# Laying out the tiles that TensorE streams and the weight blocks it holds by their addresses modulo 512

## The chip, the cores and the metric

The kernel runs on one core of a Trainium2 chip. The metric is the device time of one execution in microseconds. Three runs of the kernel before gave 626.13, 626.18 and 630.62 us, median 626.18.

## The reference

A decoder layer on 256 tokens of width 1,024 in float32, batch 1, depth 1: a SwiGLU feed-forward, a mixing block (attention and a diagonal state-space layer side by side), and a second feed-forward, each on a normalized and modulated input. Cut to what matters:

```python
ada = silu(c) @ w_ada + b_ada                       # 1024 -> 9 x 1024: shift, scale and gate, three times
h = modulate(rmsnorm(x, norm_ffn1), sh1, sc1)
x = x + 0.5 * g1 * swiglu(h, w_ffn1_in, w_ffn1_out)  # 1024 -> 2 x 2816 -> 1024
h = modulate(rmsnorm(x, norm_mix), sh2, sc2)
q, k, v, u, ga, gs = split(h @ w_in)                 # 1024 -> 4096
y_att = moba_attention(q, k, v)                      # 8 heads of 64
y_ssm = s5_mixer(u, ...)                             # 32 groups, 64 complex states each
merged = sigmoid(ga) * (y_att @ w_br_att) + sigmoid(gs) * (y_ssm @ w_br_ssm)
x = x + g2 * (merged @ w_out)
h = modulate(rmsnorm(x, norm_ffn2), sh3, sc3)
x = x + 0.5 * g3 * swiglu(h, w_ffn2_in, w_ffn2_out)
return rmsnorm(x, norm_final)
```

## The kernel before

The activations stand transposed in the on-chip buffer: 128 channels on the partitions, 256 tokens along the row, so that one block of h is 128 x 256 float32, 1,024 bytes per partition. Weights stream from memory once, in 1 MB pieces: `load` (L198) keeps four `raw` tiles of 2,048 float32 columns in flight on SyncE's queue. Each half of a raw tile, a quantum of 128 x 1,024, is split: ScalarE rounds it into `w_hi` (L239), VectorE puts the rest into `w_lo` (L247); four of each are kept. Activations are split in the same way into a high and a low part.

A product is then three matmuls (`mm3`, L269; `proj_mm`, L440): high weight with high activation, high weight with low activation, low weight with high activation. In all three a 128 x 128 block of the weight is held by TensorE and the activation of 256 columns is streamed past it; every matmul loads its own block. `tile_b` (L430) runs 24 of them for one 128-column block of an input projection, streaming h (`h_hi`, `h_lo`), and later ssm_Pr and ssm_Pi. `proj_mm` runs 24 for one quantum of an output projection, on an act tile (`a0` to `a4`, taken in turn, L543) in the feed-forwards, or on big1 and ssm_L. In one place (L1063) the roles are exchanged and 512 columns of the weight are streamed. Right behind a feed-forward or the mixing block, two projections run on the not yet normalized x (`raw_pair`, L535): their streamed rows have 258 columns, two more for the shift, and lie in four of the act tiles. The first feed-forward starts with a projection (L579) that goes along with the arrival of the weights.

The tiles come from three pools that lie one behind the other in each partition: `const` (small tables, x itself as `xT`), `near` (the names in NEAR: ssm_G0, ssm_G1, kT, qT, ssm_Pr, ssm_Pi, big0, big1, ssm_L, h_hi, h_lo, a0 to a4, in the order in which they are first asked for) and `pool` (raw, rstd, acc, diag, at_bias, w_hi, h_t, w_lo and the rest, in that order too). A tile takes its size rounded up to 32 bytes. `sb` (L62) picks the pool by the tile's name. The order of the instructions on each engine and the semaphores come from a scheduler, except in stretches marked as set by hand.

Of the kernel before, what the change touches and what calls it, by code (L numbers as in the profile page):

```python
# [10 lines left out]
F32 = mybir.dt.float32  # L11
F32R = mybir.dt.float32r
I32 = mybir.dt.int32
# [3 lines left out]
S = 256  # L17
# [21 lines left out]
ORDERED = 2  # L39
E_ = mybir.EngineType  # L40
MAN = None

NEAR = frozenset(
    ["h_hi", "h_lo", "big0", "big1", "ssm_L", "ssm_Pr", "ssm_Pi", "ssm_G0", "ssm_G1", "kT", "qT"]
    + [f"a{i}" for i in range(5)]
)
WN = 128


@with_exitstack  # L50
def kernel(ctx, tc, T, out):
    nc = tc.nc

    const = ctx.enter_context(tc.tile_pool(name="const", bufs=1))
    near = ctx.enter_context(tc.tile_pool(name="near", bufs=1))
    pool = ctx.enter_context(tc.tile_pool(name="pool", bufs=1))
    psum = ctx.enter_context(tc.tile_pool(name="psum", bufs=1, space=bass.MemoryType.PSUM))

    def bank(i):
        return psum.tile([128, 512], F32, tag=f"bank{i}", name=f"bank{i}")  # L60

    def sb(tag, shape, dt=F32, bufs=1, name=None):  # L62
        return (near if tag in NEAR else pool).tile(shape, dt, tag=tag, name=name or tag, bufs=bufs)

    x, w_ada, w_in = T["x"], T["w_ada"][0], T["w_in"][0]
    NFF = FF // 128
# [131 lines left out]
    def load():  # L198
        while state["loaded"] < len(raw_items) and (state["loaded"] < NRAW or state["loaded"] - NRAW in done):
            i = state["loaded"]  # L200
            a, b = raw_items[i][1]
            r = sb("raw", [128, 2048], bufs=NRAW)[:, 0:a * b].rearrange("p (a b) -> p a b", a=a)
            for cs, src in raw_items[i][2]:
                nc.sync.dma_start(out=r[:, :, cs], in_=src)
            raw_tiles[i] = r
            state["loaded"] += 1

    def consume_ada(i):
        v, j = raw_items[i][3:]
        r = raw_tiles.pop(i)  # L210
        if j == 0:
            acc[v] = sb("acc", [128, D], bufs=2)
        a = acc[v]
        for k in range(2):
            cs = csil[:, 2 * j + k, 0:1]
            if j == 0 and k == 0:
                nc.vector.tensor_scalar(a, r[:, k, :], cs, None, op0=ALU.mult)
            else:
                nc.vector.scalar_tensor_tensor(out=a, in0=r[:, k, :], scalar=cs, in1=a, op0=ALU.mult, op1=ALU.add)  # L219
        if j == 3:  # L220
            ada_done(v)
# [12 lines left out]
    def split_hi(k):  # L234
        i, view = quanta[k]
        r = view(raw_tiles[i])
        a, b = r.shape[1:]
        hi = sb("w_hi", [128, 1024], F32R, bufs=NSPLIT)[:, 0:a * b].rearrange("p (a b) -> p a b", a=a)
        nc.scalar.copy(hi, r)  # L239
        state["split"] += 1  # L240
        return k, r, hi
# [52 lines left out]
    ones = const.tile([128, 128], F32, name="ones")  # L294
# [4 lines left out]
    ident = const.tile([128, 128], F32, name="ident")  # L299
# [6 lines left out]
    sel = const.tile([2, 2, 64], F32, name="sel")  # L306
    cols0 = const.tile([128, 80], F32, name="cols0")
    cols = const.tile([128, 56], F32, name="cols")
    bada = cols0[:, 0:72].rearrange("p (v k) -> p v k", k=KD)
    ldt = const.tile([128, 16], F32, name="ldt")  # L310
    norm_cols = {1: cols0[:, 72:80], 4: cols[:, 32:40], 7: cols[:, 40:48]}
    hbglu = const.tile([128, 4], F32, name="hbglu")
    dq = const.tile([128, 16], F32, name="dq")
# [613 lines left out]
    dist = const.tile([128, S], F32, name="dist")  # L927

    def attn_consts():
        di = sb("dist_i", [128, S], I32)  # L930
        nc.gpsimd.iota(di, pattern=[[-1, S]], base=128, channel_multiplier=1)
        nc.vector.tensor_copy(dist, di)
        nc.gpsimd.affine_select(
            out=dist, in_=dist, compare_op=ALU.is_ge, fill=1.0e32, base=128,
            pattern=[[-1, S]], channel_multiplier=1,
        )
# [21 lines left out]
    def warm(n):  # L958
        for _ in range(n):
            nc.tensor.matmul(warm_p[:, 0:WN], ones, ones[:, 0:1].to_broadcast([128, WN]), start=True, stop=True)  # L960

# [42 lines left out]
    ssm_L = sb("ssm_L", [128, 16, 4, 32])  # L1004
# [34 lines left out]
    qT = sb("qT", [128, 4, S])  # L1039
# [4 lines left out]
    for _ in prep:  # L1044
        pass
    attn_consts()
    for j in range(4):
        if j == 2:
            raw_pair(xg, qp[1])
        p = qp[j // 2][j % 2]  # L1050
        t = sb("act_f", [128, 2, S])[:, j % 2, :]
# [32 lines left out]
    kT = sb("kT", [128, 4, S])  # L1084
# [254 lines left out]
    nf = const.tile([128, KD], F32, name="nf")  # L1339
# [85 lines left out]
```

## Time and profile before

| | |
|---|---|
| median of three runs | 626.18 us |
| the profiled execution | 629.36 us, span 627.1 us |
| mean granted TensorE clock | 0.974 of full |
| matmuls | 5,328, each with a weight load |
| read from memory | 134.82 MB, 217 GB/s over the span |

The span is the time from the first to the last instruction of the profiled execution; its whole time has what lies around it. TensorE's time is told in two parts, matmuls (PE) and weight loads (PEld), which overlap. Two neighbouring matmuls overlap too, so the length of one is more than the distance from its start to the next start, which is called its pace here. The granted clock is the share of full speed that TensorE was allowed, 1.0 in most of the span.

### The profile page before, as it was taken

To read this page: it belongs to the slowest core of one execution; us is meant where nothing else is said; L and a number is where in the kernel's file an instruction comes from. 1 tells how busy PE (TensorE), PEld (TensorE's weight loads), DVE (VectorE), ACT (ScalarE), POOL (GpSimd) and SP (SyncE) were. 2 spreads that over 40 slices of the span, in tenths; PEclk is the share of its full clock that TensorE was granted. 3 is DMA by queue.
4 is the path that set the end of the run, shared out by engine and by line. 5 is a ranking of instruction groups with operands and counts; after the bars stand their busy time and mean duration, and the time that the engine had idled before them with its cause. 6 is when DMAs were issued, how large, how long until landed. Compare 5 with 4: busy or idle time off the path is not lost. (4 is left out here: it accounts for less than half of the span.)

```text
span 627.1 us, 12786 instructions
## 1 busy us (share of the span) xinstructions
PE 607.1 (97%) x5328; PEld 580.7 (93%) x5328; DVE 455.5 (73%) x823; ACT 324.6 (52%) x535; POOL 30.6 (5%) x44
## 2 busy tenths in 40 slices
PE   7999999999999989999979999998999999999996
PEld 7888999999999989898868899997999999999995
DVE  2599999889875587999976848977974645655543
ACT  4336855487444464662456565455644343434434
POOL 6200000020000020000000000002000000000001
PEclk8999999999999997999988999998999999999998
DMA  9999989766887644785586744582576655845301
GB/s 278 319 240 332 347 281 344 251 223 239 275 281 256 203 134 135 247 291 195 172 285 214 261 153 138 198 269 83 188 265 204 244 172 192 269 149 189 133 2 68
DMA packets 97706, 136.70 MB, mean 218 GB/s; under 512 B 7697, under 2 KB 77410, under 8 KB 97648
## 3 DMA queue, kind: packets, MB, share of 16 engines
q1 hardware_dynamic: 97360, 135.81, 64.7%
q8 instruction: 42, 0.69, 0.5%
q0 software_dynamic: 288, 0.07, 0.1%
q14 instruction: 16, 0.13, 0.1%
HBM read 134.82 MB, written 1.05 MB: 217 GB/s over the span
## 5 line engine op out<-in xcount | busy, mean ns | idle before, releaser
L247 DVE TENSOR_TENSOR w_lo<-raw,w_hi 128x1024 fp32r<-128x1024 f32 (+1 forms) x184 | 223.1, 1219 | 96.0 <-ACT w_hi L239 95.4
L239 ACT CAST w_hi<-raw 128x1024 fp32r<-128x1024 f32 (+1 forms) x184 | 189.0, 1037 | 196.2 <-PE bank L271 125.7
L270 PE MATMUL bank<-h_hi,w_hi 128*128 128x256 f32 x768 | 217.7, 284 | 0.1
L271 PE MATMUL bank<-h_lo,w_hi 128*128 128x256 f32 x768 | 216.6, 282 | 0.0
L272 PE MATMUL bank<-h_hi,w_lo 128*128 128x256 f32 x768 | 216.1, 281 | 0.0
L270 PEld LDWEIGHTS bank<-h_hi,w_hi 128*128 128x128 f32 x768 | 145.6, 190 | 2.9 <-issue 2.6
L272 PEld LDWEIGHTS bank<-h_hi,w_lo 128*128 128x128 f32 x768 | 145.7, 190 | 0.9 <-issue 0.8
L271 PEld LDWEIGHTS bank<-h_lo,w_hi 128*128 128x128 f32 x768 | 145.7, 190 | 0.7 <-issue 0.7
L443 PE MATMUL bank<-a,w_hi 128*128 128x256 f32 x352 | 99.2, 282 | 0.0
L444 PE MATMUL bank<-a,w_hi 128*128 128x256 f32 x352 | 99.0, 281 | 0.0
L445 PE MATMUL bank<-a,w_lo 128*128 128x256 f32 x352 | 98.8, 281 | 0.0
L443 PEld LDWEIGHTS bank<-a,w_hi 128*128 128x128 f32 x352 | 66.3, 188 | 1.0 <-issue 1.0
L219 DVE SCALAR_TENSOR_TENSOR acc<-raw,csil,acc 128x1024 f32<-128x1024 f32 x49 | 62.7, 1279 | 6.1 <-DMA raw<-in_w_ada_dram 5.7
L445 PEld LDWEIGHTS bank<-a,w_lo 128*128 128x128 f32 x352 | 66.2, 188 | 0.0
L444 PEld LDWEIGHTS bank<-a,w_hi 128*128 128x128 f32 x352 | 66.1, 188 | 0.0
L271 PE MATMUL bank<-a,w_hi 128*128 128x258 f32 x96 | 29.1, 303 | 5.0 <-DVE a L642 5.0
L465 POOL TENSOR_TENSOR silu<-silu,act_f 128x512 f32<-128x512 f32 x7 | 9.4, 1340 | 453.1 <-ACT act_f L463 270.7
L272 PE MATMUL bank<-a,w_lo 128*128 128x258 f32 x96 | 29.3, 305 | 0.0
L270 PE MATMUL bank<-a,w_hi 128*128 128x258 f32 x96 | 28.9, 301 | 0.0
L579 PE MATMUL bank<-h_hi,w_hi 128*128 128x256 f32 x112 | 28.0, 300 | 0.5 <-ACT w_hi L239 0.5
L579 PE MATMUL bank<-h_lo,w_hi 128*128 128x256 f32 x112 | 28.0, 289 | 0.0
L579 PE MATMUL bank<-h_hi,w_lo 128*128 128x256 f32 x112 | 27.2, 282 | 0.0
(316 smaller groups left out, 828.6 us busy)
## 6 DMA issues: line engine op xcount, KB each, us to landing
raw<-in_w_ffn_in_dram SPq DMA_DIRECT2D x36, 1024.0 KB, 5.1
raw<-in_w_ada_dram SPq DMA_DIRECT2D x28, 1024.0 KB, 5.3
raw<-in_w_ffn_out_dram SPq DMA_DIRECT2D x22, 1024.0 KB, 5.0
raw<-in_w_in_dram SPq DMA_DIRECT2D x16, 1024.0 KB, 5.5
raw<-in_w_ada_dram SPq DMA_DIRECT2D x16, 512.0 KB, 7.9
raw<-in_w_ffn_in_dram SPq DMA_DIRECT2D x8, 896.0 KB, 7.5
raw<-in_w_out_dram SPq DMA_DIRECT2D x4, 1024.0 KB, 4.8
raw<-in_w_br_att_dram SPq DMA_DIRECT2D x2, 1024.0 KB, 6.1
```

The source lines that it names most:

```text
L219: nc.vector.scalar_tensor_tensor(out=a, in0=r[:, k, :], scalar=cs, in1=a, op0=ALU.mult, op1=ALU.add)
L239: nc.scalar.copy(hi, r)
L247: nc.vector.tensor_tensor(out=lo, in0=r, in1=hi.bitcast(F32), op=ALU.subtract)
L270: nc.tensor.matmul(o, st[0], mv[0], start=first, stop=False)
L271: nc.tensor.matmul(o, st[0], mv[1], start=False, stop=False)
L272: nc.tensor.matmul(o, st[1], mv[0], start=False, stop=last)
L443: nc.tensor.matmul(mm3_o, wj[0], a[0], start=first and j % 2 == 0, stop=False)
L444: nc.tensor.matmul(mm3_o, wj[0], a[1], start=False, stop=False)
L445: nc.tensor.matmul(mm3_o, wj[1], a[0], start=False, stop=last and j % 2 == 1)
L465: nc.gpsimd.tensor_tensor(out=total, in0=total, in1=sq, op=ALU.add)
L579: nc.tensor.matmul(pb[b][:, n * S:(n + 1) * S], z[:, b * 128:(b + 1) * 128], h[hl][:, kb, :], start=(kb == 0 and n == 0 and y == 0), stop= ...
```

## The change

The pools `near` and `const` are cut into parts. The streamed tiles (h_hi, h_lo, big0, big1, ssm_L, ssm_Pr, ssm_Pi and the act tiles) go into parts `str0` to `str4`, the first with a pad of 384 bytes ahead of it. Between two act tiles a part `fill0` to `fill3` takes small constants that were in `const`. Behind `str4` a part `wts` takes a pad of 32 bytes and then w_hi and w_lo, which were in `pool`. ssm_G0, ssm_G1, kT and qT go to `pool`. The integer table dist_i (L930) no longer has a tile of its own and takes one of the three slots of h_t. No other instruction is changed.

```diff
--- before.py
+++ after.py
@@ -39,11 +39,15 @@
 ORDERED = 2
 E_ = mybir.EngineType
 MAN = None
-
-NEAR = frozenset(
-    ["h_hi", "h_lo", "big0", "big1", "ssm_L", "ssm_Pr", "ssm_Pi", "ssm_G0", "ssm_G1", "kT", "qT"]
-    + [f"a{i}" for i in range(5)]
+STREAMED = ("h_hi", "h_lo", "big0", "big1", "ssm_L", "ssm_Pr", "ssm_Pi")
+FILL = (
+    ("ones", "cols0", "ada0", "ada1", "ada2", "ada3", "ada4"),
+    ("ident", "cols", "ada5", "ada6", "ada7", "ada8", "dq", "ldt"),
+    ("sel", "hbglu", "dt", "mag", "ang", "si", "co", "a_r", "a_i"),
+    ("rows1", "nf") + tuple(f"scr{i}" for i in range(7)),
 )
+PAD0 = 384
+PADW = 32
 WN = 128
 
 
@@ -51,16 +55,43 @@
 def tile_hybrid_layer_kernel(ctx, tc, T, out):
     nc = tc.nc
 
-    const = ctx.enter_context(tc.tile_pool(name="const", bufs=1))
-    near = ctx.enter_context(tc.tile_pool(name="near", bufs=1))
-    pool = ctx.enter_context(tc.tile_pool(name="pool", bufs=1))
+
+
+    parts = {}
+
+    def part(name):
+        parts[name] = ctx.enter_context(tc.tile_pool(name=name, bufs=1))
+        return parts[name]
+
+    part("const")
+    place = {}
+    for i in range(5):
+        for t in (STREAMED if i == 0 else ()) + (f"a{i}",):
+            place[t] = f"str{i}"
+        for t in FILL[i] if i < 4 else ():
+            place[t] = f"fill{i}"
+    part("str0").tile([128, PAD0 // 4], F32, name="pad0")
+    for i in range(5):
+        if i:
+            part(f"str{i}")
+        if i < 4:
+            part(f"fill{i}")
+    part("wts").tile([128, PADW // 4], F32, name="padw")
+    place.update(w_hi="wts", w_lo="wts")
+    pool = part("pool")
+
+    class Const:
+        def tile(self, shape, dt, name):
+            return parts[place.get(name, "const")].tile(shape, dt, name=name)
+
+    const = Const()
     psum = ctx.enter_context(tc.tile_pool(name="psum", bufs=1, space=bass.MemoryType.PSUM))
 
     def bank(i):
         return psum.tile([128, 512], F32, tag=f"bank{i}", name=f"bank{i}")
 
     def sb(tag, shape, dt=F32, bufs=1, name=None):
-        return (near if tag in NEAR else pool).tile(shape, dt, tag=tag, name=name or tag, bufs=bufs)
+        return parts[place.get(tag, "pool")].tile(shape, dt, tag=tag, name=name or tag, bufs=bufs)
 
     x, w_ada, w_in = T["x"], T["w_ada"][0], T["w_in"][0]
     NFF = FF // 128
@@ -927,7 +958,7 @@
     dist = const.tile([128, S], F32, name="dist")
 
     def attn_consts():
-        di = sb("dist_i", [128, S], I32)
+        di = sb("h_t", [128, S], I32, bufs=3)
         nc.gpsimd.iota(di, pattern=[[-1, S]], base=128, channel_multiplier=1)
         nc.vector.tensor_copy(dist, di)
         nc.gpsimd.affine_select(
```

## Rows read from the trace of the kernel before

**Rows 1.** The page: busy time of each engine, its share of the span, instructions

```profile
PE 607.1 (97%) x5328; PEld 580.7 (93%) x5328; DVE 455.5 (73%) x823; ACT 324.6 (52%) x535; POOL 30.6 (5%) x44
```

**Rows 2.** TensorE's waits, the longest: total us, times, longest

```profile
PE bank L271 <- DVE a L642: 5.0, 2, 2.6
```

**Rows 3.** Stretch, length, busy us (xstarted) of PE, PEld, DVE, ACT, POOL; clock, DMA, GB/s

```profile
20.00:60.00 40.00, 38.61 (x342) 33.51 (x343) 33.06 (x142) 20.84 (x39) 1.08 (x3) 1.00 1.04 293
68.00:92.00 24.00, 24.00 (x207) 24.00 (x207) 23.96 (x45) 15.22 (x29) 0.00 (x0) 1.00 0.85 290
275.00:325.00 50.00, 47.00 (x657) 42.20 (x657) 49.12 (x86) 23.92 (x51) 0.00 (x0) 1.00 0.61 208
437.00:550.00 113.00, 113.00 (x958) 112.85 (x958) 73.77 (x91) 53.60 (x65) 0.00 (x0) 1.00 0.63 215
```

**Rows 4.** The same view: a0, a1, a2, h, a4, a1, h, a3

```profile
142.35:147.95 5.60, 5.60 (x50) 5.60 (x49) 4.47 (x5) 5.50 (x10) 0.01 (x1) 1.00 0.49 167
160.36:166.02 5.66, 5.66 (x50) 5.66 (x49) 5.66 (x9) 2.62 (x3) 0.00 (x0) 1.00 0.80 280
177.22:182.97 5.76, 5.76 (x50) 5.76 (x49) 2.63 (x3) 1.76 (x3) 0.00 (x0) 1.00 0.72 277
201.18:212.38 11.20, 11.20 (x98) 11.20 (x97) 5.24 (x6) 4.69 (x5) 0.00 (x0) 1.00 0.47 143
212.38:218.02 5.64, 5.64 (x50) 5.64 (x49) 3.74 (x4) 2.62 (x3) 0.00 (x0) 1.00 0.62 193
223.62:229.06 5.44, 5.44 (x50) 5.44 (x49) 4.61 (x11) 3.67 (x7) 0.12 (x1) 1.00 0.56 176
473.55:484.86 11.31, 11.31 (x98) 11.31 (x97) 4.90 (x4) 4.69 (x5) 0.00 (x0) 1.00 0.54 184
604.78:610.47 5.69, 5.69 (x50) 5.69 (x49) 2.51 (x3) 1.57 (x2) 0.00 (x0) 1.00 0.00 0
```

**Rows 5.** The same view, 258-column projections: a0, a2, a4

```profile
445.17:446.60 1.43, 1.43 (x14) 1.43 (x13) 1.33 (x5) 1.43 (x2) 0.00 (x0) 1.00 1.03 424
448.06:449.52 1.46, 1.46 (x14) 1.46 (x13) 1.46 (x4) 0.51 (x1) 0.00 (x0) 1.00 0.06 8
245.04:246.48 1.44, 1.44 (x14) 1.44 (x13) 1.44 (x6) 0.82 (x3) 0.00 (x0) 1.00 0.05 15
```

**Rows 6.** Matmul groups: line, out<-in, shape, count, busy us, mean ns

```profile
L270 PE MATMUL bank<-h_hi,w_hi 128*128 128x256 f32 x768 | 217.7, 284 | 0.1
L443 PE MATMUL bank<-a,w_hi 128*128 128x256 f32 x352 | 99.2, 282 | 0.0
L270 PE MATMUL bank<-a,w_hi 128*128 128x258 f32 x96 | 28.9, 301 | 0.0
L579 PE MATMUL bank<-h_hi,w_hi 128*128 128x256 f32 x112 | 28.0, 300 | 0.5 <-ACT w_hi L239 0.5
```

**Rows 7.** One line's matmuls in a window: ns min/median/max, starts

```profile
L444 PE MATMUL bank<-a,w_hi x17: 276/276/280, 223.4 to 228.8; 128*128 128x256 f32 x17
L271 PE MATMUL bank<-h_lo,w_hi x32: 277/279/281, 201.3 to 212.2; 128*128 128x256 f32 x32
L272 PE MATMUL bank<-h_hi,w_lo x1: 274/274/274, 270.2 to 270.2; 128*128 128x256 f32 x1
L837 PE MATMUL bank<-ident,big x32: 270/272/327, 98.4 to 122.8; 128*128 128x128 f32 x32
L270 PE MATMUL bank<-h_hi,w_hi x83: 277/280/388, 275.3 to 320.6; 128*128 128x256 f32 x83
```

**Rows 8.** Instructions in order of time: start us, us, engine, line

```profile
225.10 0.28 PE L444 MATMUL bank<-a,w_hi 128*128 128x256 f32 x1
225.10 0.19 PEld L445 LDWEIGHTS bank<-a,w_lo 128*128 128x128 f32 x1
```

**Rows 9.** Instructions of dist_i and of h_t, as in rows 7

```profile
L931 POOL IOTA dist_i<- x1: 353/353/353, 3.4 to 3.4; 128x256 int32 x1
L417 DVE SCALAR_TENSOR_TENSOR h_t<-xT,ada,at_bias x24: 472/478/486, 14.3 to 449.9; 128x256 f32<-128x256 f32 x24
```

## The prediction

> **What bounds the kernel.** I read the page's engine line first: TensorE is busy 97% of the span [rows 1]. Then the list of who waited for whom: its longest wait on another engine sums to 5.0 us [rows 2]. So nothing feeds TensorE late, and only the rate at which it takes matmuls can be worth much. The page's mean of 280 ns for one matmul is its length; matmuls overlap, so their pace has to come from windows that hold one sort of matmul alone. An output quantum is 16 each of L443, L444 and L445, so 48 matmuls on one act tile start in each 5.4 to 5.8 us window of [rows 4] (the counts there include two that reach in from an edge); four input quanta on h are 96. Which act tile it is follows from the code, which hands them out in turn.
>
> Window by matmuls gives: a0 5.60/48 = 116.7 ns, a1 117.9, a2 120.0, a3 118.5, a4 117.5, h 116.7 in one stretch and 117.8 in another, and a1 once 113.3 [rows 4]. The DMA shares and the ScalarE and VectorE times in those rows go up and down without the pace following them: a3 with no DMA at all is slower than a0 with half of it. What distinguishes the tiles is where they lie.
>
> **Where the operands lie, from the code.** Tiles stand in the order in which they are first asked for, rounded up to 32 bytes. In `near` all sizes are multiples of 512 up to the act tiles of 4,128 bytes (258 columns, 16 bytes each). If h lies at R modulo 512, so do ssm_G, big, ssm_L, ssm_Pr, ssm_Pi and a0, and a1 to a4 lie at R+32 to R+128. Behind a4 stand four raw tiles (multiples of 512), two rstd (64 bytes), two acc, diag and at_bias: w_hi and w_lo lie at R+160+64 = R+224, and each of their 128-column blocks is 512 bytes, so all blocks do. The block thus lies above the streamed tile by 224 bytes for h and a0, 192 for a1, 160 for a2, 128 for a3, 96 for a4. In that order the paces are 116.7 to 117.8, 117.9 (once 113.3), 120.0, 118.5, 117.5: highest at 160, falling on both sides. The projections on raw x, 258 columns, show the same order: 12 matmuls in 1.43, 1.46 and 1.44 us on a0, a2 and a4, that is 119, 122 and 120 ns [rows 5]. Their rows are 1,032 bytes long, so a4's distances there run from 96 down to 72.
>
> **The change, part by part.** *The distance becomes 64 everywhere.* const loses the small tiles; the streamed ones start behind a 384-byte pad; each act tile (4,128) is followed by 992 bytes of filling (512+320+5x32, 512+224+4x32+64+64, 512+32+7x64, 512+32+7x64), which makes 5,120, a multiple of 512. So h, big, ssm_L, ssm_Pr, ssm_Pi and a0 to a4 share one residue; behind a4 (32 over) the 32-byte pad puts w_hi and w_lo 64 above it. No matmul, split or load of weights is added or taken away.
>
> What is 64 worth? No row shows it at this pairing, so it is bounded from both sides. Below: the a1 window at 113.3 has the same code, tile and distance as windows at 117.9, so some 4.5 ns of a matmul can go. Its matmuls last 276 ns against 279 on h; where the load behind a matmul on h is of ssm_G, at distance 0, the matmul lasted 274 [rows 7], 2 ns less again, which makes 111.3 the lower bound. Above: a2's 120.0. The nearest rows argue for opposite ends: distance 0 (274 ns) for a free stream, a4's 72 to 96 in the raw projections (120 ns, no better than a0's 119) for no gain. Transposes of big, which lies 64 above ident, decide nothing: their 128 columns last 272 ns, as long as 256 do here [rows 7]. I take 113.3: 64 is nearer to 0 than to a4's 96 or the peak at 160, and near 0 both reads begin almost together (a matmul and the load for the next start within 10 ns of each other [rows 8]) and the stream, moving twice as far in the same time (1,024 bytes against 512), runs away from the block, while from farther below it has to overtake it (an argument, which no row shows).
>
> *How many matmuls gain.* Streamed through weights: 3x768 on h, 3x352 on a, 3x112 in the first projection and 3x96 of 258 columns [rows 6]; from the code 3x64 on big and ssm_L and 3x32 on ssm_Pr and ssm_Pi; together 4,272. Left out: the 336 of L579, which run while DMA is at 1.04 and above; some 120 after them up to 92 us (207 start in the stretch from 68, the first 85 still of L579), and 3x83 between 275 and 325 us, stages in which VectorE is busy 23.96 of 24.00 and 49.12 of 50.00 us [rows 3, 7] and would take over as the bound. That leaves about 3,566: some 2,270 on h and its like, 1,008 on a, 288 of 258 columns.
>
> *The sum.* h from 117.2 (middle of its two paces) to 113.3: 2,270 x 3.9 = 8.9 us. a from 118.1 (mean of 116.7, 117.9, 120.0, 118.5, 117.5) to 113.3: 1,008 x 4.8 = 4.8 us. Raw projections by some 5 ns: 288 x 5 = 1.4 us. Together 15.1 us. The profiled execution took 629.4 us (span 627.1), 3.2 more than the median of 626.2; taken from it the sum gives 614.3, from the median **611.1**. What would be late next: VectorE, at 73.77 of 113.00 us, and DMA, at 0.63, have room in the longest stage [rows 3].
>
> *dist_i moves into a slot of h_t.* Its iota (353 ns) ran on GpSimd at 3.4 us [rows 9], with VectorE's cast behind it, while x was still landing; the first h_t is written at 14.3 us [rows 9], so a slot is free then: 0. If the iota were put behind h_t's other users, the cast would hold VectorE's queue, and the splits behind it, for 0.35 us and the semaphores: under 1 us. *Constants, ident, ssm_G, kT, qT and raw at new addresses*: same instructions, so 0; at most some 3 ns, what tile and tile differ by above, on the 1,056 other matmuls of 5,328 [rows 1], 3 us either way.
>
> *A rule against it.* The window rows show a pace that differs from tile to tile, 116.7 against 120.0, with the same matmul. The Trainium skill, "TensorE: Matmul & The Clock Gate", in the step-by-step of a matmul, says that the moving operand and the weight load have two independent read ports and that loading the next weights takes no bandwidth from the running matmul. By that rule no distance could matter and the sum would be 0, 626.2 us; the trace does not agree as far as tiles go, since a2 costs 3.3 ns more than a0.
>
> **The rivals.** *Levelled only (same):* 64 is no better than 224, and all the change does is to bring a1 to a4 to h's pace. For it: a4 at 96 runs at h's pace (117.5), and in the raw rows at 96 to 72 a4 is no faster than a0 at 224. Price: 1,008 x 0.9 + 288 x 1.4 = 1.3 us, 624.9. *No effect (same):* the pace depends on something other than the distance; a1's two paces at one distance speak for it, the order of the tiles in both tables against. 626.2. This is also what the page's rule above would give. *A worse meeting (slower):* at 64 the two reads meet as at 160, and every stream runs at a2's pace. Price: 2,270 x 2.8 + 1,008 x 1.9 + 288 x 1.5 = 8.7 us, 634.9. It decides from a rise of 1.8 ns on 3,566 matmuls, 6.3 us, that is from 119.2 ns on h. For it: the paces are not monotonic in distance, and 64 was never tried; against: falling from 160 to 96.
>
> **Numbers.** Free stream 0.47, levelled only 0.27, no effect 0.09, worse meeting 0.17. The likeliest gives 611, its own range 603 (111.3 ns, and the left-out stages gain too) to 619 (half the gain). The whole range: 600, the lower bound on all 4,272 (x 6.1 = 26 us), to 631, which holds both cases of no change and a worse meeting of about 1.4 ns; it leaves out most of the slower case. A measurement of this kernel can tell about 1%, 6.3 us, from no change: faster 0.47, same 0.36, slower 0.17.
>
> **What would show it.** Windows of 48 on any act tile should last the same for a0 to a4, near 5.44 us, and four quanta on h 10.9 instead of 11.2; matmuls should last 274 to 276 ns. All tiles alike at 5.60 to 5.65 would mean levelling, 5.76 the worse meeting, and tiles that still differ among themselves would mean that distance modulo 512 is not what sets the pace. VectorE should idle less between 92 and 236 us. The prediction fails most simply if 64 still lies inside the reach of whatever makes 96 no better than 224.

## The result, and the profile after

The changed kernel took 624.0 us (median of 20 runs, 619.4 to 629.2), the kernel before 626.7 us beside it (20 runs, 624.1 to 631.7). The ratio is 0.994 with a 95% interval of 0.992 to 0.996: some 3 us were gained, which is real and less than 1%. The forecast was 611. The profiled execution of the changed kernel happens to be the longest of its 20 (629.18 us, span 626.9), so its total shows no gain over the profiled one before (span 627.1); it has to be read stage by stage. Line numbers are 31 higher than before.

The engine line of the page, which answers to [rows 1]:

```profile
PE 602.9 (96%) x5328; PEld 575.3 (92%) x5328; DVE 455.2 (73%) x823; ACT 325.1 (52%) x535; POOL 31.1 (5%) x44
```

TensorE is busy 4.2 us less (607.1 before), and in this execution it waits that much more. Its longest waits, to be held against [rows 2] (engine, line, what it waited for: us in total, times, longest):

```profile
PE bank L302 <- DVE a L673: 4.8, 2, 2.4
PE bank L1180 <- issue: 3.6, 2, 3.3
PE bank L399 <- DMA raw<-in_w_ada_dram: 2.6, 2, 1.6
PE bank L610 <- ACT h_hi L451: 2.3, 2, 1.7
```

The last two lie in the first stage, which goes along with the arrival of the weights. Now the windows of [rows 4] and one of [rows 5] in the changed kernel: a0, a1, a2, h, a4, a1, a1, a3, h, h, a3, with 48 matmuls on an act tile and 96 on h, and then a2 and a0 with 12 matmuls of 258 columns (columns as in [rows 3]):

```profile
142.70:148.14 5.44, 5.44 (x51) 5.44 (x49) 4.73 (x6) 5.32 (x10) 0.13 (x1) 1.00 0.47 164
160.32:165.97 5.65, 5.65 (x50) 5.65 (x49) 5.65 (x9) 2.58 (x3) 0.00 (x0) 1.00 0.86 284
178.12:183.56 5.44, 5.44 (x51) 5.44 (x49) 0.73 (x1) 1.05 (x1) 0.00 (x0) 1.00 0.99 368
201.99:213.29 11.30, 11.30 (x98) 11.30 (x97) 5.23 (x6) 4.69 (x5) 0.00 (x0) 1.00 0.52 160
213.29:218.94 5.65, 5.65 (x50) 5.65 (x49) 3.74 (x4) 2.62 (x3) 0.00 (x0) 1.00 0.60 188
224.60:230.25 5.65, 5.65 (x50) 5.65 (x49) 4.79 (x11) 3.88 (x8) 0.35 (x1) 1.00 0.57 191
485.83:491.48 5.65, 5.65 (x51) 5.65 (x49) 3.74 (x4) 2.62 (x3) 0.00 (x0) 1.00 0.58 196
519.90:525.34 5.44, 5.44 (x50) 5.44 (x49) 3.74 (x4) 2.62 (x3) 0.00 (x0) 1.00 0.51 161
525.34:536.22 10.88, 10.88 (x98) 10.88 (x97) 6.68 (x6) 4.71 (x5) 0.00 (x0) 1.00 0.58 194
559.32:570.62 11.30, 11.30 (x98) 11.30 (x97) 4.90 (x4) 4.69 (x5) 0.00 (x0) 1.00 0.50 160
604.54:610.20 5.66, 5.66 (x51) 5.66 (x49) 2.51 (x3) 1.57 (x2) 0.00 (x0) 1.00 0.00 0
...
437.57:439.01 1.44, 1.44 (x15) 1.44 (x13) 1.44 (x4) 1.43 (x4) 0.00 (x0) 1.00 0.04 11
446.17:447.61 1.44, 1.44 (x15) 1.44 (x13) 1.40 (x5) 1.44 (x2) 0.00 (x0) 1.00 1.02 421
```

In these windows two paces are left, and nothing between: 5.44/48 = 113.3 ns and 5.65/48 = 117.8. Both occur on one tile (a3 at 519.90 and at 604.54) and on h (525.34 and 559.32), so the tile no longer decides. Such a steady pace is called a rhythm here, and the first matmul behind an interruption of the stream a restart. The two rhythms hold for whole uninterrupted stretches: read from the start times of the matmuls, 452 to 514 us is 527 matmuls at 117.8, 515 to 556 is 358 at 113.3, 557 to 612 is 469 at 117.8 again. The 120.0 of a2 is gone. The raw projections stay at 1.44/12 = 120 ns. One line's matmuls in the a1 window of 224.60 and in the a3 window of 519.90 tell the two paces apart by their length (ns min/median/max, first and last start):

```profile
L475 PE MATMUL bank<-a,w_hi x16: 281/281/281, 224.4 to 229.7; 128*128 128x256 f32 x16
...
L475 PE MATMUL bank<-a,w_hi x16: 276/276/276, 520.0 to 525.1; 128*128 128x256 f32 x16
```

### The profile page after: what moved, and what is told of

It reads as the page before. It is cut to its first block, busy times and chain, and to the rows that moved or that the text cites. A ratio compares the mean times of both kernels' runs of the same rounds, so it can differ in the third digit from the quotient of the medians.

```text
span 626.9 us, 12787 instructions
## 1 busy us (share of the span) xinstructions
PE 602.9 (96%) x5328; PEld 575.3 (92%) x5328; DVE 455.2 (73%) x823; ACT 325.1 (52%) x535; POOL 31.1 (5%) x44
```

## The experiments

Two rivals stood beside the reading that 64 bytes allows two rhythms and that a restart picks one: that levelling the act tiles brought all of the gain, and that distance doesn't matter. A triple is the three matmuls of one product, a residue an address modulo 512, and a distance how far the held block lies above the streamed tile. In the code and the diffs, `...` stands for lines left out.

**Triples alone, all distances.** The kernel `sweep` only loads two streamed and two held tiles and runs the triple of `mm3`, 48 matmuls at a time:

```python
for s in SHIFTS:            # (96, 0): streamed tiles at residue 224, then 128
    for d in DISTS:         # range(0, 512, 32): held blocks d bytes above them
        for f in KICKS:     # (0, 1, 2, 3): what stands ahead of the 48
            ...
                nc.tensor.matmul(o[:, 0:c], a[:, q:q + 128], b[:, p:p + c], start=t == 0, stop=t == RUN - 1)
```

> Leaves out the whole layer: it only runs the matmul triples of the kernel (held high, high, low block; streamed high, low, high tile; 256 columns) 48 at a time, for the distances 0, 32, ... 480 bytes modulo 512 between held and streamed blocks, with the streamed tiles at two residues (224 and 128), each four times with another restart ahead of it (nothing, one matmul of 4 columns in plain float32, a shorter second matmul, two plain float32 matmuls). Two rhythms (the theory): every run of 48 goes at one of two paces, 113.3 or 117.8 ns; which of them are found depends on the distance, and for one distance on the restart; at 64 both occur, and there are distances at which only one does. Distances 128 and 160 show a third, 119 to 120 ns. The residue of the streamed tile itself changes nothing. Distance alone (rival 1): each distance has one pace, whatever the restart, with 64 somewhere between 113.3 and 117.8. Residue (rival 2): the two residues 224 and 128 give different paces at the same distance. No effect of addresses (rival 3): all 128 runs go at one pace within 0.5 ns.

Windows of 36 paces at residue 224 (columns as above). In order: distance 0; 64 twice; 96; 128; 160; 192 twice; 224 twice; 256; 320:

```profile
28.20:32.52 4.32, 4.32 (x39) 4.32 (x38) 0.00 (x0) 0.00 (x0) 0.00 (x0) 1.00 0.00 0
63.86:67.94 4.08, 4.08 (x38) 4.08 (x37) 0.00 (x0) 0.00 (x0) 0.00 (x0) 1.00 0.00 0
81.35:85.59 4.24, 4.24 (x39) 4.24 (x38) 0.00 (x0) 0.00 (x0) 0.00 (x0) 1.00 0.02 4
86.99:91.22 4.23, 4.23 (x38) 4.23 (x37) 0.00 (x0) 0.00 (x0) 0.00 (x0) 1.00 0.00 0
110.53:114.80 4.27, 4.27 (x39) 4.27 (x37) 0.00 (x0) 0.00 (x0) 0.00 (x0) 1.00 0.00 0
145.93:150.25 4.32, 4.32 (x39) 4.32 (x38) 0.00 (x0) 0.00 (x0) 0.00 (x0) 1.00 0.02 4
158.02:162.10 4.08, 4.08 (x39) 4.08 (x37) 0.00 (x0) 0.00 (x0) 0.00 (x0) 1.00 0.02 4
175.70:179.94 4.24, 4.24 (x39) 4.24 (x38) 0.00 (x0) 0.00 (x0) 0.00 (x0) 1.00 0.01 4
181.35:185.59 4.24, 4.24 (x39) 4.24 (x37) 0.00 (x0) 0.00 (x0) 0.00 (x0) 1.00 0.00 0
192.82:197.02 4.20, 4.20 (x38) 4.20 (x37) 0.00 (x0) 0.00 (x0) 0.00 (x0) 1.00 0.00 0
216.42:220.74 4.32, 4.32 (x38) 4.32 (x37) 0.00 (x0) 0.00 (x0) 0.00 (x0) 1.00 0.00 0
252.09:256.17 4.08, 4.08 (x38) 4.08 (x37) 0.00 (x0) 0.00 (x0) 0.00 (x0) 1.00 0.02 4
```

Divided by 36 this is 120.0 at 0, 113.3 or 117.8 at 64, 117.5 at 96, 118.6 at 128, 120.0 at 160, 113.3 or 117.8 at 192, 117.8 or 116.7 at 224. VectorE and ScalarE stand still and DMA all but does (a share of 0.02 at most), so what differs is the addresses and the restart alone. This is the table of [rows 4]: 120.0 on a2 at 160, 118.5 on a3 at 128, 117.5 on a4 at 96, 116.7 and 117.8 on h and a0 at 224, and the 117.9 and the single 113.3 on a1 at 192, which the prediction had used as its lower bound. One window of the kernel before, which [rows 4] leave out, has a3 at another pace, 5.76/48 = 120.0 (columns as in [rows 3]):

```profile
519.02:524.78 5.76, 5.76 (x50) 5.76 (x49) 3.74 (x4) 2.62 (x3) 0.00 (x0) 1.00 0.53 177
```

At distance 128 the triples alone have this pace too, behind one of four restarts at residue 128. The theory holds in its main point, that a distance allows certain rhythms and 64 two. It had not said that distances 256 apart are alike (0 and 256, 64 and 320), so that the period is 256 bytes and not 512, nor that 0 is as slow as 160; and it was wrong that every run but those at 128 and 160 goes at 113.3 or 117.8: 32 had 118.3 and 224 mostly 116.7. Between residues 224 and 128 the set of paces is the same at 0, 32, 64, 160 and 192; at 96 and 128 the second one shows 120.0 beside the others, and at 224 it shows 116.7 alone. Whether the residue does that or the pace of the run ahead was not separated. No effect of addresses and one pace per distance are both out; distance 32 gave 118.3.

**What picks the rhythm.** The kernel `kick` has the same triples: 33 distances in steps of 8 bytes, then distance 64 with an extra matmul of 0 to 192 columns ahead of each run of 24.

```python
if k:
    nc.tensor.matmul(banks[7][:, 0:k], st[1][:, s0:s0 + 128], mv[0][:, m0:m0 + k], start=True, stop=True)
```

> Leaves out the layer, as the first measurement of matmul triples did. First 33 distances from 0 to 256 bytes in steps of 8, each with four runs of 24 matmuls that follow an extra matmul of 0, 32, 96 or 160 columns into another bank. Then, at distance 64 alone, 104 runs of 24 in mixed order, each behind an extra matmul of 0, 4, 16, 32, 64, 96, 128 or 192 columns, 13 times each. Two rhythms, set by the restart (the theory): at 64 a run without an extra matmul keeps the pace of the run before it; an extra matmul moves it from 113.3 to 117.8 ns or back, the same way each time for one length and one pace before; a length that leads from either pace to 113.3 may exist. Of the distances between 32 and 96 some have only 113.3 (then that is where the tiles should lie) or none but 64 has it. Chance (rival): after an extra matmul of one length, from one pace, both paces follow about equally often, and 113.3 can be lost without any restart.

Windows of 12 paces: distance 8; then, at 64, runs that follow one another, behind extra matmuls of 4, 192, 0 and 96 columns:

```profile
27.90:29.28 1.38, 1.38 (x14) 1.38 (x13) 0.00 (x0) 0.00 (x0) 0.00 (x0) 1.00 0.00 0
463.09:464.50 1.41, 1.41 (x14) 1.41 (x13) 0.00 (x0) 0.00 (x0) 0.00 (x0) 1.00 0.00 0
466.01:467.37 1.36, 1.36 (x15) 1.36 (x13) 0.00 (x0) 0.00 (x0) 0.00 (x0) 1.00 0.00 0
468.73:470.09 1.36, 1.36 (x15) 1.36 (x13) 0.00 (x0) 0.00 (x0) 0.00 (x0) 1.00 0.00 0
471.61:473.02 1.41, 1.41 (x14) 1.41 (x13) 0.00 (x0) 0.00 (x0) 0.00 (x0) 1.00 0.00 0
```

117.8, then 113.3 behind the 192 columns, kept where nothing comes between (13 of 13 runs without an extra matmul keep the pace before them), and lost behind 96 columns. Over the 104 runs 113.3 was lost behind every extra matmul of 4 to 128 columns (28 of 28; the expectation of *Three distances* has this number wrong) and kept behind every one of 192 (4 of 4); from 117.8 it was found in 23 of 49 with 4 to 128 columns and 5 of 9 with 192. So the restart picks. Away from 113.3 it does so always the same way; from 117.8 one length led both ways, which the theory had excluded and its rival, chance, had not. No distance in steps of 8 had 113.3 behind all of its four restarts; 8 bytes gave 115.6 every time.

**Levelled at 224.** One number of the changed kernel is undone: the act tiles stay level, the distance goes back.

```diff
-PADW = 32
+PADW = 192
```

> One number of the changed kernel is set otherwise: the pad ahead of w_hi and w_lo is 192 bytes in place of 32, so every streamed tile lies 224 bytes below the held blocks, as h and a0 did before, and a0 to a4 are still level. Two rhythms (the theory, by which 64 gives long stretches at 113.3 ns and 224 gives 116.7 or 117.8): a1 to a4 come down to h's pace, h stays; 1,008 x 0.9 + 288 x 1.4 = 1.3 us less than before, ratio 0.998, that is slower than the changed kernel by some 2.4 us; no window of 48 on an act tile goes under 5.60 us but by chance. Levelling only (rival): all that the change brought is from a1 to a4 no longer lying at 96 to 192; ratio 0.994 as for the changed kernel, windows of 48 at 5.60 to 5.65. Distance doesn't matter at all: 1.000.

628.6 us against 628.9, ratio 0.998 (0.994 to 1.002). Windows on a1, a2 and a3:

```profile
162.56:168.16 5.60, 5.60 (x51) 5.60 (x50) 5.60 (x9) 2.63 (x3) 0.00 (x0) 1.00 0.83 264
503.02:508.62 5.60, 5.60 (x51) 5.60 (x49) 3.74 (x4) 2.62 (x3) 0.00 (x0) 1.00 0.58 189
605.40:611.00 5.60, 5.60 (x50) 5.60 (x49) 2.51 (x3) 1.57 (x2) 0.00 (x0) 1.00 0.00 0
```

116.7 on all act tiles (of the stretches of over 200 matmuls, read from the start times, those from 70 and 381 us were at 117.8, the others at 116.7): levelling works as the prediction's second case has it and is worth, as far as the interval tells, what that case said (1.3 us). The interval reaches the changed kernel's 0.994, so the times alone don't part the two; the windows do, since 113.3 is gone.

**Level at 0.** `PADW = 480` instead.

> The changed kernel with the pad ahead of w_hi and w_lo at 480 bytes in place of 32: held blocks and streamed tiles lie at one residue, distance 0 modulo 512. In the measurement of triples alone distance 0 gave 120.0 ns behind every restart. Theory (distance sets which rhythms there are, in the layer as in the triples alone): windows of 48 on any act tile last 5.76 us, four quanta on h 11.52; against the kernel before, mean 117.4 on 4,072 matmuls of 256 and 258 columns, 2.6 x 4,072 = 10.5 us more, less what stages that wait for data hide, so 8 to 10.5 us, ratio 1.013 to 1.017. Rival (levelling is all that counts): as the changed kernel, 0.994. Rival (the prediction's own argument, that the closer to 0 the freer the stream): 113.3 everywhere, 0.975.

632.4 us against 629.0, ratio 1.007 (1.004 to 1.010). Windows on a1, a1 and a3:

```profile
162.57:168.33 5.76, 5.76 (x51) 5.76 (x50) 5.58 (x8) 2.62 (x3) 0.00 (x0) 1.00 0.85 310
483.90:489.66 5.76, 5.76 (x51) 5.76 (x49) 3.74 (x4) 2.61 (x3) 0.00 (x0) 1.00 0.59 204
606.40:612.16 5.76, 5.76 (x50) 5.76 (x49) 2.51 (x3) 1.57 (x2) 0.00 (x0) 1.00 0.00 0
```

120.0 everywhere, as in the triples alone, and the sign is right; the price is not. The mean pace rose from 117.44 to 119.90 ns, which on the 4,072 matmuls of 256 and 258 columns that ran without an interruption at full clock makes 10.0 us; by the ratio 4.5 came. Part of the rest is clock: the mean granted clock was 0.989 over its 10 runs and 0.981 over the 23 of the kernel before. The two levels being 1 and 0.5, that is 14 us at half clock instead of 24. A line through those 23 runs gives 0.35 us of time for each us at half clock, so by it 3.5 us were given back. The remaining 2 us were not traced.

**The integer table alone.** The kernel before, with the diff's last hunk only: `di = sb("h_t", [128, S], I32, bufs=3)`.

> The kernel before with one part of the change alone: the integer table takes a slot of h_t; no address of a streamed or held tile is moved by it. Theory (the part is worth nothing that can be measured; the few instructions of GpSimd and VectorE that move past one another lie where TensorE has its work): ratio 1.000, within 0.002. Rival (the table's cast, now behind other users of the slot, holds VectorE's queue and with it the splits of the first stage, which after the change is some 2 us behind by 55 us): 2 to 4.7 us more, 1.003 to 1.007.

628.4 us against 629.0, ratio 0.999 (0.996 to 1.002): worth nothing that can be measured.

**An extra matmul at restarts.** The changed kernel, with 21 matmuls of 192 columns whose result is overwritten at once:

```diff
-    def tile_b(o, w, h, nk, c0=0):
+    def tile_b(o, w, h, nk, c0=0, extra=False):
         hi, lo = w
+        if extra:
+            nc.tensor.matmul(o[:, 0:192], hi[:, 0, c0:c0 + 128], h[0][:, 0, 0:192], start=True, stop=True)
...
-                        tile_b(p[:, n * S:(n + 1) * S], nextq(), h, KD)
+                        tile_b(p[:, n * S:(n + 1) * S], nextq(), h, KD, extra=p is pg and n == 0)
...
-            tile_b(p[:, c * S:(c + 1) * S], w, ya, 4, c * 128)
+            tile_b(p[:, c * S:(c + 1) * S], w, ya, 4, c * 128, extra=c == 0)
```

> The changed kernel, distance 64, with 21 extra matmuls of 192 columns that are overwritten at once: ahead of the first matmul of each group of four projections in the feed-forwards and of four in the mixing block. In the triples alone such a matmul led from 117.8 ns to 113.3 in 5 of 9 cases and left 113.3 as it was in 4 of 4. Theory (the rhythm is picked at each restart and kept; the gain that was missing is the stretches that start in the slow one, 1,747 matmuls in five long stretches): two thirds of 1,747 x 4.45 = 7.8 us come back, 5.2 us, less 21 x 0.116 = 2.4 us that the extra matmuls take; 2.8 us faster than the changed kernel, ratio to the kernel before 0.990, and most windows of 48 on act tiles between 440 and 610 us at 5.44. Rival (the pace has to do with what else goes on in the stretch, not with its start): stretches keep their paces, 2.4 us slower than the changed kernel, 0.998.

617.9 us against 629.0, ratio 0.983 (0.979 to 0.987). Windows on a1, a1, a1 and a3:

```profile
161.26:166.91 5.65, 5.65 (x50) 5.65 (x49) 5.61 (x8) 2.31 (x3) 0.00 (x0) 1.00 1.03 372
223.66:229.10 5.44, 5.44 (x50) 5.44 (x49) 4.60 (x11) 3.67 (x7) 0.12 (x1) 1.00 0.59 197
477.17:482.61 5.44, 5.44 (x50) 5.44 (x49) 3.74 (x4) 2.62 (x3) 0.00 (x0) 1.00 0.62 206
593.91:599.35 5.44, 5.44 (x50) 5.44 (x49) 2.51 (x3) 1.57 (x2) 0.00 (x0) 1.00 0.00 0
```

Work was added, and the kernel became faster than the kernel before and the changed one (ratio 0.994). By the start times 7 of the extra matmuls met a stream at 117.8, and 6 of them led to 113.3; 11 met one at 113.3, and all kept it. The stretch that was 452 to 514 us in the changed kernel turned at its first extra matmul and stayed at 113.3; the one from 158 us turned only at its second, at 184 us. It is faster than the theory's 0.990, because nearly all long stretches turned and not two thirds. That the paces belong to what else goes on in a stretch is out.

**Three distances.** In a triple three matmuls and three loads alternate, so three distances are free. The kernel `combo` tries 8 x 8 x 8 of them, each behind two restarts, with

```python
a = st[0][:, q:q + 128] if y < 2 else st[1][:, q + f // 4:q + f // 4 + 128]
b = mv[1][:, p + e // 4:p + e // 4 + 256] if y == 1 else mv[0][:, p:p + 256]
```

> Leaves out the layer, as the other measurements of triples do. Three distances are set apart from one another, each 0 to 224 bytes in steps of 32: held high block above streamed high tile, streamed low tile above streamed high tile, held low block above held high block; so far the two others were 0. Each of the 512 combinations runs 21 triples' matmuls twice, behind an extra matmul of 96 and of 128 columns (of 21 runs at 113.3 ns in the measurement with mixed order that were followed by an extra matmul of 4 to 128 columns all but none fell to 117.8). Theory (each of the three matmuls of a triple meets the load running beside it by its own distance, and the rhythm is what the three settle to): some combinations keep 113.3 or less behind both restarts, others are at 120 and above; (64, 0, 0) comes out at 113.3 or 117.8 by the restart. Rival: only the first distance counts; all 64 combinations that share it have its paces, and none keeps 113.3 always.

Windows of 12 paces: held high 64 above, held low no farther, behind both restarts; held low another 128 farther, behind both:

```profile
685.98:687.34 1.36, 1.36 (x15) 1.36 (x14) 0.00 (x0) 0.00 (x0) 0.00 (x0) 1.00 0.00 0
688.50:689.91 1.41, 1.41 (x14) 1.41 (x13) 0.00 (x0) 0.00 (x0) 0.00 (x0) 1.00 0.05 12
706.64:708.00 1.36, 1.36 (x15) 1.36 (x14) 0.00 (x0) 0.00 (x0) 0.00 (x0) 1.00 0.00 0
709.14:710.50 1.36, 1.36 (x14) 1.36 (x13) 0.00 (x0) 0.00 (x0) 0.00 (x0) 1.00 0.00 0
```

Of 512 combinations only (64, 0, 128) ran at 113.3 behind both, and only (64, 0, 0) behind one. About half of all lie at 117.9 or above. So the first distance does not settle the pace: of the 64 combinations that share 64 as the first, 62 never had 113.3, and with (64, 0, 32) the same triples ran at 118.9 behind the first restart.

**The held low blocks 128 bytes farther.** The changed kernel with that one pad, and beside it the changed kernel itself:

```diff
-    place.update(w_hi="wts", w_lo="wts")
+    part("wtl").tile([128, 32], F32, name="padl")
+    place.update(w_hi="wts", w_lo="wtl")
```

> The changed kernel with one pad more: 128 bytes between w_hi and w_lo, so that the held high blocks lie 64 bytes above the streamed tiles and the held low blocks 192 above them. No instruction is added. In the triples alone this was the one of 512 combinations that went at 113.3 ns behind both restarts. Theory (the rhythm that a stretch settles to is set by the three distances of the triple, and the missing gain is the stretches in the slow rhythm): every long stretch goes at 113.3, windows of 48 on any act tile last 5.44 us, four quanta on h 10.88; against the kernel before the 15.1 us of the prediction's sum less some for stages that don't gain, ratio 0.977 to 0.982, and some 8 us less than the changed kernel. Rival (restarts decide in the layer whatever the distances): a mix of 113.3 and 117.8 remains, ratio 0.990 to 0.997. Rival (a faster stream is given back by more half-clock time, as the slower one at distance 0 got some back): windows at 5.44, but mean clock under 0.975 and ratio 0.983 to 0.990.

> The changed kernel itself once more, on the same chip as the kernel with the extra pad. Ratio 0.994 within 0.002; long stretches at 113.3 and 117.8 mixed, and the same ones as in the first profile if what comes before a stretch picks the rhythm, others if chance does.

617.0 us against 627.6 for the kernel before, ratio 0.983 (0.978 to 0.988); the changed kernel beside it took 623.7, ratio 0.994 (0.991 to 0.997). No instruction more, and 6.7 us less than the changed kernel. Windows on a1, a1 and a3, then the first 12 and the next 12 paces of the stretch that starts at 443.75 us, and the engine line:

```profile
158.67:164.11 5.44, 5.44 (x51) 5.44 (x49) 5.44 (x9) 2.18 (x3) 0.00 (x0) 1.00 0.89 280
219.82:225.26 5.44, 5.44 (x50) 5.44 (x49) 4.61 (x11) 3.67 (x7) 0.13 (x1) 1.00 0.59 203
592.35:597.79 5.44, 5.44 (x51) 5.44 (x49) 2.52 (x3) 1.57 (x2) 0.00 (x0) 1.00 0.00 0
443.75:445.16 1.41, 1.41 (x14) 1.41 (x13) 1.41 (x5) 1.41 (x3) 0.00 (x0) 1.00 1.02 415
445.16:446.52 1.36, 1.36 (x14) 1.36 (x13) 1.36 (x4) 0.51 (x1) 0.00 (x0) 1.00 0.28 105
```

```profile
PE 591.7 (96%) x5328; PEld 565.0 (92%) x5328; DVE 455.3 (74%) x823; ACT 324.9 (53%) x535; POOL 31.0 (5%) x44
```

Every stretch of over 250 matmuls is at 113.3 to 113.5. It is not that the restarts went better: as in the last two rows of windows (117.5 ns, then 113.3), most stretches begin slowly, and all 13 of 46 matmuls and more have come down to 113.3 by their 19th pace. The slow rhythm, which the changed kernel held for 527 matmuls, does not last at these distances. The clock did not take the gain back: 0.9805 on average against 0.982.

Of the changed kernel's repetition the long stretches from 157, 198, 374, 446 and 551 us were at 117.8 and those from 133 and 508 at 113.3, as in the first profile; where in the first a wait for w_lo cut the one from 158 at 175 us and 113.3 followed, here nothing cut it and it stayed at 117.8. Two shorter ones came out the other way round than in the first profile: 47 matmuls from 127 us at 113.4 in place of 117.8, and 60 from 293 us at 117.8 in place of 113.5. So what precedes a stretch mostly picks the same rhythm for it, and not always.

## Why the prediction was wrong, step by step

**The place of the cost was right.** TensorE's pace on streamed matmuls bounds the kernel; it depends on how far the held block lies from the streamed tile; five distances explain the five tiles. The triples alone show it.

**The failing step is "What is 64 worth? ... I take 113.3".** 113.3 was taken as the pace of a distance, while it is one of two rhythms that 64 allows, and 64 had it in 36 to 39% of the matmuls on h and the act tiles (the share of those closer than 115.2 ns; 31 to 38% in the repetition). The evidence was in [rows 4], a1 with two paces at one distance, and a3 had two as well, the second in the window that the rows leave out. The text used a1's lower pace as a bound for what can go, and the pair as a point for *no effect*, and never asked what decides between them. The terms of the sum, with the mean paces from the start times in the three traces (matmuls at full clock without an interruption) and the prediction's counts:

| | matmuls | forecast | measured | with the extra pad |
|---|---|---|---|---|
| h and its like | 2,270 | 117.2 to 113.3, 8.9 us | 117.0 to 116.1, 2.1 us | 113.9, 7.0 us |
| act tiles | 1,008 | 118.1 to 113.3, 4.8 us | 117.9 to 116.2, 1.7 us | 113.7, 4.3 us |
| raw, 258 columns | 288 | 5 ns, 1.4 us | 120.5 to 119.7, 0.2 us | 120.1, 0.1 us |
| sum | 3,566 | 15.1 us | 4.0 us | 11.4 us |

4.0 us agrees with the 0.6% of the ratio, and 11.4 with the 10.6 us that the extra pad brought (617.0 against 627.6). The sum was thus worked out rightly for a kernel that keeps the fast rhythm, but for the raw projections; the change made one that has it in some stretches, by the restart. One count is off and costs 0.2 us: of the 207 matmuls from 68 us on 35 are of L579, not 85, and 48 on an act tile, so that the prediction's h is 48 too many.

**The argument for 64 was false.** "64 is nearer to 0" and "near 0 both reads begin almost together" would make 0 the best distance; it is one of the worst, 120.0 in the triples and in the layer. The 274 ns of the one matmul ahead of a load of ssm_G [rows 7] was one value, of another tile, and not a steady pace. That the pace falls on both sides of 160 was read from five points and continued to 64; in the triples it goes 118.3, 113.3 or 117.8, 117.3 to 120.0, 118.6 to 120.0, 120.0 from 32 to 160, with no slope.

**The modulus was too large.** Distances repeat after 256 bytes. It changed no number here.

**Raw projections.** The four rows of 1,032 bytes in one act tile lie 64, 56, 48 and 40 bytes below the held blocks, and levelling the first one left them at 120 ns. In the triples of 256 columns, with both streamed tiles at one distance, 56, 48 and 40 gave 117.8 and more behind each of four restarts; the mix of the four was not measured. The 1.4 us were the mean's gain put on tiles that have 64 in one row of four.

**The table's place.** The prediction has its iota at 3.4 us, where a slot is free. It went behind h_t's other users (instructions of the table in the changed kernel, columns as in [rows 9]):

```profile
L962 POOL IOTA h_t<- x1: 343/343/343, 55.5 to 55.5; 128x256 int32 x1
...
L963 DVE CAST dist<-h_t x1: 282/282/282, 72.4 to 72.4; 128x256 f32<-128x256 int32 x1
```

The prediction named this as the other possibility, at under 1 us; the run with this part alone shows 0.999.

**The rule against it.** With VectorE and ScalarE idle and DMA all but idle, the same matmuls went at 113.3 to 120.0 ns by addresses alone. The Trainium skill, "TensorE: Matmul & The Clock Gate", in "Step-by-step: what each phase is for", gives TensorE two independent read ports, one for the streamed and one for the held operand. By that rule, as the prediction read it, the kernel before and all of these would take the same time; the runs differ by 15 us, from 617.0 to 632.4 (ratios 0.983 and 1.007), so for this pairing the runs decide against it.

**The chances.** *Levelled only* names 624.9, close to what came by luck and for another reason: with the distance at 224 and levelled tiles 113.3 is gone and the ratio is 0.998. The true case, a distance with two rhythms, was not among the four. It lies between *free stream* and *levelled only*, and the range held it. Of the signs, matmuls of 276 ns came in the fast stretches, and windows that differ came too; the prediction would have read these as distance having no part, and *Levelled at 224* and *Level at 0* show that it has one.

## What to carry to other kernels

Where TensorE loads a block for every matmul, look at the pace (start to start) and not at the length, and if equal work shows two paces, find out what chooses before pricing the better one. Try the layout on the bare pattern first: one small kernel gave the paces of 16 distances, and another the one combination of three (streamed tiles at R, held high at R+64, held low at R+192, modulo 256) that had the best pace behind both restarts tried, which then was worth 1.7% in the layer. A layout that only allows a good pace is worth the share of stretches that take it; look for one in which the slow pace does not last.

## What was not expected of the hardware

- 256-column matmuls with a load each settle to steady paces, among them 113.3, 115.6, 116.7, 117.8 and 120.0 ns. Which of them a layout allows depends on three distances modulo 256 bytes, and an extra matmul of 4 columns ahead can change it. At distance 64 both paces lasted until something interrupted the stream (527 matmuls in the longest stretch); with the held low blocks 128 bytes farther only 113.3 did.
- A kernel with a slower stream spent less time at half clock (0.989 of full against 0.981), which by the line through the runs of the kernel before is some 3.5 us; the faster one with the extra pad did not spend more (0.9805 against 0.982). Why is open.
- That the read of the streamed tile and the load of the next block meet somewhere in the on-chip buffer is the natural reading of these numbers, and stays an argument: no run shows the place. Why 192 columns keep the fast rhythm and 96 lose it is open too.
